# Where the outputs of a two-layer matmul kernel stand on chip, and how its last outputs leave it

## The chip, the cores and the metric

The kernel runs on one core of one Trainium2 chip. The metric is the device time of one execution in microseconds (us). Every ratio is the mean time of one kernel's runs over that of the other's of the same rounds, so it is not quite the ratio of the medians quoted beside it. A profile is of one execution. Its span leaves out some 1.6 us of that execution's time (900.2 of 901.8 us before).

## The reference

```python
x: (16, 512, 768)   w1: (768, 3072)   b1: (3072)   w2: (3072, 768)      # float32
y = np.maximum(np.matmul(x, w1) + b1, 0)
return np.matmul(y, w2).astype(np.float32)
```

## The kernel before

The 8192 rows of x are taken in eight blocks of 1024. The hidden dimension is cut into two chunks of 1536, so there are 16 block passes ("it" 0 to 15): first all eight blocks with chunk 0, then all eight with chunk 1. Passes are called blocks 0 to 15 below. Both products use fast matrix multiplication schemes: seven products in place of eight for x·w1, and 20 products of sums of y and sums of w2 for y·w2. All matmuls are fp16. VectorE forms the sums, VectorE and ScalarE take the products out of PSUM.

The second product of a block is a list of 20 steps. Each "mm" is eight matmuls into two PSUM banks (q0 to q3), and what follows takes them into the buffers s0 to s5 or into one of eight outputs of 128x768 fp32. Its end:

```python
    ("mm", 10, 2, False), ("DVE", "q1", 2, 1, "s5", 1), ("DVE", "o5", 1, -1, "s2", 1),
    ("mm", 14, 0, False), ("ACT", "s4", 0, -1),
    ("mm", 9, 3, False),  ("DVE", "q1", 3, -1, "s4", 1), ("DVE", "o7", 1, 1, "s1", -1),
    ("mm", 17, 2, False), ("DVE", "o4", 2, 1, "s5", 1),
    ("mm", 0, 0, False),  ("DVE", "o1", 0, 1, "s3", -1),
    ("mm", 7, 3, False),  ("DVE", "o6", 3, -1, "s4", 1),     # o6 = s4 - q3
```

Outputs o2, o3 and o0 come earlier in the list. An output stands in one of four buffers until its store has read it. In the first eight blocks it is stored plainly. In the last eight it is added to what lies in DRAM by an accumulating store from GpSimd:

```python
        self.o_pool = pool("o", 4)
        ...
        def output(to):
            pair = {"o5": 0, "o7": 0, "o1": 1, "o6": 1}.get(to)
            if it <= self.NSB or pair is None:                    # NSB = 8
                return self.o_pool.tile([P, 2, NH], FP32, name="o")
            ...                                # blocks 9 to 15: two larger tiles for o5, o7, o1, o6
        def total(engine, to, q, sign, kept=None, kept_sign=None):
            ...
            if to[0] == "o":
                ...
                if it < self.NSB:
                    nc.sync.dma_start(out=rows, in_=o)
                else:
                    nc.gpsimd.dma_start(out=rows, in_=o, accum_op=ALU.add)
```

The next block's first product starts between the last two steps of this list. Its step p1 writes the PSUM bank that o7 was taken from. Its step p5 writes the bank that o4 was taken from, and ScalarE copies it into the buffer that the second product calls s4. Its step p3 adds onto that bank after the copy.

x stands in slots of 128x1536 fp16, four slots for the even blocks, four for the odd ones, three for sums:

```python
        self.x = self.one.tile([P, 11, 3, self.MH], FP16, name="x")
        self.s = self.one.tile([P, 6, self.N], FP32, name="s")
```

Of the kernel before, what the change touches and what calls it, by code (L numbers as in the profile page):

```python
# [9 lines left out]
FP32 = mybir.dt.float32  # L10
# [3 lines left out]
ALU = mybir.AluOpType  # L14
# [4 lines left out]
P = 128  # L19
# [20 lines left out]
U_OF = (A1, A3, D106, D102, A10, A4, A2, A11, A0, A7, D103, A5, D101, A6, D105, U15, A9, A8,  # L40
        D104, D100)
# [108 lines left out]
class Fast:  # L150
# [440 lines left out]
        return [p1, p5, p6, p2, p7, p3, p4]  # L591


    def second(self, it):

        nc = self.nc
        QM, NH = self.QM, self.NH
        row0 = (it % self.NSB) * 2 * self.MH

        def product(p, q, start):  # L600
            for s in range(4):
                for j in range(2):
                    m0 = s * QM + j * P
                    nc.tensor.matmul(self.ps[:, 2 * q + j, 0:NH],  # L604
                                     lhsT=self.y[:, U_OF[p], m0:m0 + P],
                                     rhs=self.v[:, V_OF[p], s, :], start=(start and s == 0),
                                     stop=(s == 3), skip_group_check=True)

        def at(name):
            if name[0] == "q":  # L610
                q = int(name[1])
                return self.ps[:, 2 * q:2 * q + 2, 0:NH]
            return self.s[:, int(name[1])].rearrange("p (a n) -> p a n", a=2)

        pairs = {}

        def output(to):

            pair = {"o5": 0, "o7": 0, "o1": 1, "o6": 1}.get(to)
            if it <= self.NSB or pair is None:  # L620
                return self.o_pool.tile([P, 2, NH], FP32, name="o")
            if pair not in pairs:
                pairs[pair] = [self.raw_pool.tile([P, 4, NH], FP32, name="o2", tag="raw"), 0]
            half = pairs[pair][1]
            pairs[pair][1] = 2
            return pairs[pair][0][:, half:half + 2]

        def total(engine, to, q, sign, kept=None, kept_sign=None):
            ps = at(f"q{q}")
            o = output(to) if to[0] == "o" else at(to)  # L630
            if kept is None:
                if engine == "ACT":
                    nc.scalar.activation(out=o, in_=ps, func=ACTF.Copy, scale=float(sign))  # L633
                else:
                    nc.vector.tensor_scalar(out=o, in0=ps, scalar1=float(sign), scalar2=None,
                                            op0=ALU.mult)
            else:
                a, b = (ps, at(kept)) if sign > 0 else (at(kept), ps)
                nc.vector.tensor_tensor(out=o, in0=a, in1=b,  # L639
                                        op=ALU.add if sign == kept_sign else ALU.subtract)  # L640
            if to[0] == "o":
                r, n = divmod(int(to[1]), 2)
                rows = self.of[row0 + r * QM:row0 + (r + 1) * QM, n * NH:(n + 1) * NH]
                rows = rows.rearrange("(j p) n -> p j n", p=P)
                if it < self.NSB:
                    nc.sync.dma_start(out=rows, in_=o)
                else:
                    nc.gpsimd.dma_start(out=rows, in_=o, accum_op=ALU.add)  # L648

        steps = []  # L650
        for what in SECOND:
            if what[0] == "mm":
                steps.append([lambda a=what[1:]: product(*a)])
            else:
                steps[-1].append(lambda a=what: total(*a))
        return [lambda fns=fns: [fn() for fn in fns] for fns in steps]
# [92 lines left out]
    def plan(self):  # L749

        TP, NSB, NIT = self.TP, self.NSB, self.NIT
        self.hooks = {}
        vector = self.nc.vector

        def put(kind, it, q, i, fn, *args):
            self.hooks.setdefault((kind, it, q, i), []).append(lambda: fn(*args))


        put("p1", 0, 1, 1, self.transpose_x_first, 1)
        for s in range(4):  # L760
            put("p1", 0, 2, s, self.square_x, 0, 0, s, True)
            put("p1", 0, 1, 2, self.square_x, 0, 1, s)
        put("p1", 0, 1, 2, self.load_x, 1, (1,))
        put("p1", 0, 4, 1, self.transpose_x, 1, 0)
        put("p1", 0, 5, 1, self.transpose_x, 1, 1)
        put("m2", 0, 0, 3, self.save_x, 0, 0)
        for t, at in enumerate(((1, 1), (1, 2), (2, 0), (2, 2), (3, 1), (4, 0))):
            put("p1", 0, *at, lambda t: self.sums_w1(self.w1s[t], vector, (0, 1, 2)), t)
        for t in range(TP):
            put("m2", 0, 0, 8 + t, lambda t: self.sums_w1(self.w1s[t], vector, (3,)), t)  # L770
        for n in range(15):
            put("p1", 0, 2 + n // 8, n % 8 // 2, self.sum_w2, n, 0, 2)
            late = {10: 3, 12: 4, 14: 5, 13: 6, 11: 7}.get(n)
            at = ("m2", 0, 0, late) if late else ("p1", 0, 4 + (n + 2) // 8, (n + 2) % 8 // 2)
            put(*at, self.sum_w2, n, 2, 4)
        put("m2", 0, 0, 12, self.sum_w2, 15)

        for it in range(NIT):
            nxt = it + 1
            if nxt < NSB:  # L780
                for half in range(2):
                    if it:
                        put("m1", it, 2 + half, 0, self.transpose_x, nxt, half)
                    for s in range(4):
                        put("m2", it, 0, 1 + 4 * half + s, self.square_x, nxt, half, s)
                if nxt + 1 < NSB:
                    put("m2", it, 0, 5, self.load_x, nxt + 1, (0,))
                    put("m2", it, 0, 9, self.load_x, nxt + 1, (1,))
                put("m1", nxt, 1, 0, self.save_x, nxt, 1)
                put("m1", nxt, 4, 0, self.save_x, nxt, 0)  # L790
            elif nxt < NIT:
                put("m1", it, 4 if nxt == NSB + 1 else 2, 4, self.fetch_x, nxt, 0)
            if nxt <= NSB:
                for n, i in enumerate((6, 7, 14)):
                    put("m2", it, 0, i, self.sums_x, nxt, n)
            elif nxt < NIT:
                put("m2", it, 0, 1, self.fetch_x, nxt, 1)

        last = NSB - 1
        for t in range(TP):  # L800
            for step, at in enumerate((("m2", 1 + t, 0, 1), ("m2", 1 + t, 0, 13),
                                       ("m1", 2 + t, 0, 3))):
                put(*at, self.ahead_w1, 1 + t, t, step)
            put("m1", last, t, 6, self.fetch_w1, t)
        for n in range(12):
            put("m1", 1 + n // 3, 3 + n % 3, 0, self.load_w2,
                self.w2dram.rearrange("p b (s n) -> p b s n", s=4)[:, n // 4 * 2:][:, 0:2], 1,
                n // 4, n % 4)
        for q, at in ((2, ("m1", last, 1, 6)), (0, ("m1", last, 3, 6)), (1, ("m2", last, 0, 1))):
            put(*at, self.fetch_w2_aside, q)  # L810
        put("m2", last, 0, 9, self.fetch_w2, B0)
        put("m2", last, 0, 13, self.fetch_w2, B2)
        for n, at in ((2, ("m2", last, 0, 12)), (6, ("m2", last, 0, 14)),
                      (1, ("m2", last, 0, 16)), (15, ("m2", last, 0, 17)),
                      (9, ("m2", last, 0, 17)), (7, ("m2", last, 0, 18)),
                      (3, ("m1", NSB, 0, 3)), (0, ("m1", NSB, 1, 1)), (8, ("m1", NSB, 1, 2)),
                      (4, ("m1", NSB, 1, 3)), (5, ("m1", NSB, 2, 1)), (12, ("m1", NSB, 2, 3)),
                      (10, ("m2", NSB, 0, 5)), (14, ("m2", NSB, 0, 6)),
                      (13, ("m2", NSB, 0, 11)), (11, ("m2", NSB, 0, 14))):
            put(*at, self.sum_w2, n)  # L820

        for t in range(TP):
            for n in range(3):
                put("m2", 1 + t, 0, 11 + 3 * n, self.stat_w1, 0, t, n)
                put("m2", NSB + t // 2, 0, 3 + 9 * (t % 2) + 2 * n, self.stat_w1, 1, t, n)
        for n in range(8):
            put("m1", 2 + n // 2, 2 + 2 * (n % 2), 3, self.stat_w2, 0, n // 2, n % 2)
            put("m1", NSB + 1 + n // 4, 1 + n % 4, 3, self.stat_w2, 1, n // 2, n % 2)
        for stage in range(3):
            put("m1", NSB + 3 + stage, 5, 6, self.out_of_range, stage)  # L830
# [51 lines left out]
```

## Time and profile before

| | before |
|---|---|
| time, four runs | 901.62, 902.07, 904.03, 906.7 us |
| span and granted TensorE clock of the profile | 900.2 us, 0.994 |
| TensorE busy | 868.4 us (96%) |
| last matmul to the end of the span | 14.2 us |

L536 is the first product (L604 is the second). Timelines give start, duration, engine, line, operation, operands, count, and idle time before. One matmul of L536 shows 379 ns (the profile works out the ends of matmuls by a model; their starts are measured), though they start 0.216 us apart: each overlaps the next. TensorE's timeline at the end of block 0 (start, duration, engine, line, operation, operands, count, and idle time before) shows it:

```profile
71.90 0.81 PE L536 MATMUL ps<-x,w1s 128*128 128x512 f16 x3 [0.25 <-DVE o L639]
72.54 1.46 PE L604 MATMUL ps<-v,y 128*128 128x384 f16 x8
73.84 2.75 PE L536 MATMUL ps<-x,w1s 128*128 128x512 f16 x12
78.60 2.75 PE L536 MATMUL ps<-x,w1s 128*128 128x512 f16 x12 [2.00 <-ACT s L544]
```

### The profile page before, as it was taken

How to read it: one execution, taken by the hardware profiler on the slowest of the kernel's cores; microseconds unless marked ns; L12 is line 12 of the kernel's file. 1: busy time of each engine (PE TensorE's matmuls, PEld its weight loads, DVE VectorE, ACT ScalarE, POOL GpSimd, SP SyncE). 2: the span in 40 equal slices, each digit the busy share in tenths (PEclk: the TensorE clock that was granted, in tenths of full speed). 3: DMA queues.
4: the chain of work that ended last, by engine and by line, in shares of the span. 5: the costliest groups of instructions: out<-in, count | busy, mean ns of one | idle time of the engine just before them, and what ended most of it. 6: DMA issues, size and time to landing. Idle time of an engine off the chain costs nothing.

```text
span 900.2 us, 12564 instructions
## 1 busy us (share of the span) xinstructions
PE 868.4 (96%) x4677; PEld 458.1 (51%) x4677; DVE 618.4 (69%) x1081; ACT 519.5 (58%) x791; POOL 190.9 (21%) x173
## 2 busy tenths in 40 slices
PE   8998999999999999999989999999999999999993
PEld 6454554545445455454545545455454545545452
DVE  2896856768577675866798666676766668576663
ACT  4764757757577675666346586775626354362630
POOL 6210150501404032040200401203030130402113
PEclk9999999999999999999999999999999999999997
DMA  9999498795986959539543716639273573815418
GB/s 205 199 209 261 101 230 231 117 274 125 268 191 136 263 109 262 134 142 348 226 168 140 110 32 160 104 125 138 76 126 63 155 109 123 125 38 93 81 19 124
DMA packets 120325, 138.11 MB, mean 153 GB/s; under 512 B 67116, under 2 KB 113732, under 8 KB 116420
## 3 DMA queue, kind: packets, MB, share of 16 engines
q0 software_dynamic: 50672, 46.41, 36.5%
q1 hardware_dynamic: 69264, 90.06, 30.4%
q8 instruction: 38, 0.62, 0.3%
q10 hardware_dynamic: 324, 0.80, 0.3%
q14 instruction: 27, 0.22, 0.1%
HBM read 72.17 MB, written 77.66 MB: 166 GB/s over the span
## 4 chain that ended last, share of the span: by engine, by line
PE 40%; issue 36%; POOL 9%; DVE 6%; DMA 6%; ACT 2%; POOLq 0%; DVEq 0%; ACTq 0%
PE ps L536 23%; PE ps L604 18%; POOL out_dram L648 8%; DMA out_dram<-o 3%; DVE o L639 3%; DMA v<-in_w_dram 2%; DVE ps L639 1%; DVE v L338 1%; DMA w1s<-in_w_dram 1%; ACT s L633 1%; ACT s L544 1%; POOL w1s L277 1%; DVE y L468 0%; DVE w1s L285 0%; DVE x L391 0%
## 5 line engine op out<-in xcount | busy, mean ns | idle before, releaser
L536 PE MATMUL ps<-x,w1s 128*128 128x512 f16 x1890 | 416.2, 379 | 11.7 <-ACT s L544 8.8
L604 PE MATMUL ps<-v,y 128*128 128x384 f16 x2560 | 424.6, 326 | 2.5 <-DVE y L468 1.9
L604 PEld LDWEIGHTS <-y 128*128 128x128 f16 x2560 | 249.5, 98 | 174.4 <-ACT y L553 2.5
L536 PEld LDWEIGHTS <-w1s 128*128 128x128 f16 x1890 | 184.8, 98 | 232.4 <-issue 15.4
L544 ACT ACTIVATE s<-ps,b1y 128x512 f32<-128x512 f32 x210 | 142.0, 687 | 162.4 <-DVE y L548 53.9
L468 DVE TENSOR_TENSOR y<-y 128x512 f16<-128x512 f16 x512 | 201.8, 420 | 32.9 <-ACT y L553 25.6
L548 DVE CUSTOM_DVE_ANT_0 y<-ps,s 128x512 f16<-128x512 f32 x210 | 145.0, 690 | 107.4 <-PE ps L536 73.2
L648 POOL DMA_DIRECT2D out_dram<-o x64 | 77.8, 1380 | 366.0 <-DVE o L639 366.0
L633 ACT ACTIVATE s<-ps 128x768 f32<-128x768 f32 x96 | 77.7, 810 | 121.2 <-PE ps L604 96.7
L639 DVE TENSOR_TENSOR o<-s,ps 128x768 f32<-128x768 f32 x64 | 61.0, 953 | 60.1 <-PE ps L604 26.7
L639 DVE TENSOR_TENSOR s<-ps,s 128x768 f32<-128x768 f32 x96 | 90.2, 954 | 12.5 <-ACT s L633 6.5
L553 ACT ACTIVATE y<-ps,b1y 128x512 f16<-128x512 f32 x90 | 61.9, 687 | 39.7 <-PE ps L536 39.7
L639 DVE TENSOR_TENSOR o<-ps,s 128x768 f32<-128x768 f32 x64 | 58.8, 953 | 36.8 <-ACT s L633 34.9
L394 POOL TENSOR_TENSOR x<-x 128x3072 f16<-128x3072 f16 x7 | 42.1, 6009 | 65.7 <-DVE x L391 53.1
L382 ACT ACTIVATE scrap<-xn 128x768 f16<-128x768 f16 x60 | 50.3, 838 | 0.8
L277 POOL DMA_DIRECT2D x<-in_w_dram x12 | 10.1, 848 | 182.7 <-PE ps L536 182.7
L559 ACT ACTIVATE ps<-ps,b1y 128x512 f32<-128x512 f32 x60 | 39.6, 659 | 10.8 <-PE ps L536 7.9
L553 ACT ACTIVATE y<-ps 128x512 f16<-128x512 f32 x60 | 35.8, 597 | 0.0
L346 ACT ACTIVATE scrap<-scrap 128x1536 f16<-128x1536 f16 x24 | 35.4, 1477 | 0.1
L633 ACT ACTIVATE ps<-ps 128x768 f32<-128x768 f32 x32 | 25.5, 798 | 9.2 <-PE ps L604 8.9
L486 PE MATMUL ps<-x,w1s 128*128 128x512 f16 x132 | 28.8, 379 | 0.4 <-DVE x L441 0.2
L369 POOL DMA_DIRECT2D xn<-in_x_dram x15 | 11.5, 764 | 74.3 <-ACT scrap L382 73.5
(64 smaller groups left out, 260.2 us busy)
## 6 DMA issues: line engine op xcount, KB each, us to landing
out_dram<-o SPq DMA_DIRECT2D x64, 384.0 KB, 4.3
out_dram<-o POOLq DMA_DIRECT2D x64, 384.0 KB, 5.8
xd<-x SPq DMA_DIRECT2D x8, 1536.0 KB, 5.4
x<-xd SPq DMA_DIRECT2D x8, 1536.0 KB, 8.4
xn<-in_x_dram POOLq DMA_DIRECT2D x15, 768.0 KB, 7.3
xd<-x SPq DMA_DIRECT2D x7, 1152.0 KB, 7.0
x<-xd SPq DMA_DIRECT2D x7, 1152.0 KB, 5.3
w1d<-x SPq DMA_DIRECT2D x6, 672.0 KB, 5.3
```

The costliest lines, as they stand in the source:

```text
L382: self.nc.scalar.activation(out=self.junk(self.K), in_=rows, func=ACTF.Square, accum_out=self.stat[:, i:i + 1])
L394: (self.nc.gpsimd if it > 1 else self.nc.vector).tensor_tensor(out=x[:, a21:self.XS2 + 1:self.XS2 - a21], in0=x[:, a21:self.XS1 + 1:self.X ...
L468: self.nc.vector.tensor_tensor(out=pair(*outs), in0=pair(*ins0), in1=pair(*ins1), op=ALU.add if sign > 0 else ALU.subtract)
L536: nc.tensor.matmul(ps, lhsT=w[:, slot, k, :], rhs=x[:, xslot, k, :], start=(start and k == 0), stop=(k == 2), skip_group_check=True)
L544: nc.scalar.activation(out=kept(name), in_=ps, func=ACTF.Identity, bias=bias)
L548: nc.vector._custom_dve(TENSOR_ADD_SAT, out=self.y_of(self.TP * half + t, m), in0=self.two(ps), in1=self.two(kept(name)), s0=F_MAX, s1=0.0)
L553: nc.scalar.activation(out=self.y_of(self.TP * half + t, m), in_=self.two(ps), func=ACTF.Relu, **kw)
L559: nc.scalar.activation(out=g["b"], in_=g["a"], func=ACTF.Identity, bias=bias1)
L604: nc.tensor.matmul(self.ps[:, 2 * q + j, 0:NH], lhsT=self.y[:, U_OF[p], m0:m0 + P], rhs=self.v[:, V_OF[p], s, :], start=(start and s == 0) ...
L633: nc.scalar.activation(out=o, in_=ps, func=ACTF.Copy, scale=float(sign))
L639: nc.vector.tensor_tensor(out=o, in0=a, in1=b, op=ALU.add if sign == kept_sign else ALU.subtract)
L648: nc.gpsimd.dma_start(out=rows, in_=o, accum_op=ALU.add)
```

## The change

Its intent is threefold: to have no output wait for a buffer in blocks 0 to 8, to take VectorE's other work out of the crowded places, and to end the program with plain stores. Two of eight outputs of a block (o5, o4) are put into slots of x that the block no longer needs. For four of the eight last outputs the part of chunk 0 is loaded from DRAM beforehand and added by GpSimd to the s buffer that the output will be formed from, so these leave by plain stores. The last output is split into halves on two queues.

```diff
+    def x_outputs(self, slot):
+        o = self.x[:, slot].rearrange("p k m -> p (k m)").bitcast(FP32)
+        return o.rearrange("p (a n) -> p a n", a=2)
+    LAST = {"o7": ("s1", -1, 3), "o4": ("s5", 1, 15), "o1": ("s3", -1, 12), "o6": ("s4", 1, 16)}
+    def fetch_last(self, to):                    # slot = index in LAST
+        self.nc.sync.dma_start(out=self.x_outputs(slot), in_=self.rows_of(self.NIT - 1, to))
+    def add_last(self, to):
+        self.nc.gpsimd.tensor_tensor(out=s, in0=s, in1=self.x_outputs(slot),
+                                     op=ALU.add if sign > 0 else ALU.subtract)
 ...
         def output(to):
+            slot = {"o5": 2, "o4": 3}.get(to)
+            if it <= self.NSB and slot is not None:
+                return self.x_outputs(4 * (it % 2) + slot)
 ...
+            if final and to == SECOND[-1][1]:
+                for j, queue in enumerate((nc.scalar, nc.sync)):
+                    nc.vector.tensor_tensor(out=o[:, j], in0=at(kept)[:, j], in1=ps[:, j], op=ALU.subtract)
+                    queue.dma_start(out=self.rows_of(it, to)[:, j], in_=o[:, j])
+                return
 ...
-                if it < self.NSB:
+                if it < self.NSB or (final and to in self.LAST):
                     nc.sync.dma_start(out=rows, in_=o)
 ...
-        for t, at in enumerate(((1, 1), (1, 2), (2, 0), (2, 2), (3, 1), (4, 0))):    # sums of w1
+        for t, at in enumerate(((1, 1), (1, 2), (2, 0), (2, 2))):
+        for t in (4, 5):
+            put("m1", 1, t - 3, 3, lambda t: self.sums_w1(self.w1s[t], vector), t)
 ...   # and the fourth sum of these two strips no longer in block 0's second product
-                for n, i in enumerate((6, 7, 14)):
-                    put("m2", it, 0, i, self.sums_x, nxt, n)
+                put("m2", it, 0, 6, self.sums_x, nxt, 0)
+                put("m2", it, 0, 7, self.sums_x, nxt, 1)
+                put("m1", nxt, 0, 0, self.sums_x, nxt, 2)                # this is L399
 ...   # sums of w2 for chunk 1, six of them moved:
-  (6, ("m2", last, 0, 14)), (1, ("m2", last, 0, 16)), (9, ("m2", last, 0, 17)), (7, ("m2", last, 0, 18))
+  (6, ("m1", NSB, 1, 0)),   (1, ("m1", NSB, 4, 3)),   (9, ("m2", NSB, 0, 1)),   (7, ("m2", NSB, 0, 3))
-  (13, ("m2", NSB, 0, 11)), (11, ("m2", NSB, 0, 14))
+  (13, ("m2", NSB, 0, 9)),  (11, ("m2", NSB, 0, 12))
+        for to, (_, _, i) in self.LAST.items():
+            put("m1", NIT - 1, 1, 6, self.fetch_last, to)
+            put("m2", NIT - 1, 0, i, self.add_last, to)
```

More of the change, by code (lines that the diff above doesn't have):

```diff
@@ L591, in first, with rows_of @@
         return [p1, p5, p6, p2, p7, p3, p4]
+    def rows_of(self, it, to):
+        r, n = divmod(int(to[1]), 2)
+        m0 = (it % self.NSB) * 2 * self.MH + r * self.QM
+        rows = self.of[m0:m0 + self.QM, n * self.NH:(n + 1) * self.NH]
+        return rows.rearrange("(j p) n -> p j n", p=P)
+    def x_outputs(self, slot):
[3 more added lines that the diff above has]
+    def fetch_last(self, to):
+        slot = list(self.LAST).index(to)
+        self.nc.sync.dma_start(out=self.x_outputs(slot), in_=self.rows_of(self.NIT - 1, to))
+    def add_last(self, to):
+        slot = list(self.LAST).index(to)
+        name, sign, _ = self.LAST[to]
+        s = self.s[:, int(name[1])].rearrange("p (a n) -> p a n", a=2)
+        self.nc.gpsimd.tensor_tensor(out=s, in0=s, in1=self.x_outputs(slot),
+                                     op=ALU.add if sign > 0 else ALU.subtract)
     def second(self, it):
@@ L597, in second @@
         QM, NH = self.QM, self.NH
-        row0 = (it % self.NSB) * 2 * self.MH
+        final = it == self.NIT - 1
         def product(p, q, start):
-            for s in range(4):
-                for j in range(2):
-                    m0 = s * QM + j * P
-                    nc.tensor.matmul(self.ps[:, 2 * q + j, 0:NH],
-                                     lhsT=self.y[:, U_OF[p], m0:m0 + P],
-                                     rhs=self.v[:, V_OF[p], s, :], start=(start and s == 0),
-                                     stop=(s == 3), skip_group_check=True)
+            order = [(s, j) for s in range(4) for j in range(2)]
+            if final and p == SECOND[-2][1]:
+                order.sort(key=lambda sj: sj[1])
+            for s, j in order:
+                m0 = s * QM + j * P
+                nc.tensor.matmul(self.ps[:, 2 * q + j, 0:NH],
+                                 lhsT=self.y[:, U_OF[p], m0:m0 + P],
+                                 rhs=self.v[:, V_OF[p], s, :], start=(start and s == 0),
+                                 stop=(s == 3), skip_group_check=True)
         def at(name):
@@ L630, in total @@
             o = output(to) if to[0] == "o" else at(to)
+            if final and to == SECOND[-1][1]:
+                for j, queue in enumerate((nc.scalar, nc.sync)):
+                    nc.vector.tensor_tensor(out=o[:, j], in0=at(kept)[:, j], in1=ps[:, j],
+                                            op=ALU.subtract)
+                    queue.dma_start(out=self.rows_of(it, to)[:, j], in_=o[:, j])
+                return
             if kept is None:
@@ L641, in total @@
             if to[0] == "o":
-                r, n = divmod(int(to[1]), 2)
-                rows = self.of[row0 + r * QM:row0 + (r + 1) * QM, n * NH:(n + 1) * NH]
-                rows = rows.rearrange("(j p) n -> p j n", p=P)
-                if it < self.NSB:
+                rows = self.rows_of(it, to)
+                if it < self.NSB or (final and to in self.LAST):
                     nc.sync.dma_start(out=rows, in_=o)
@@ L766, in plan @@
         put("m2", 0, 0, 3, self.save_x, 0, 0)
-        for t, at in enumerate(((1, 1), (1, 2), (2, 0), (2, 2), (3, 1), (4, 0))):
+        for t, at in enumerate(((1, 1), (1, 2), (2, 0), (2, 2))):
             put("p1", 0, *at, lambda t: self.sums_w1(self.w1s[t], vector, (0, 1, 2)), t)
-        for t in range(TP):
             put("m2", 0, 0, 8 + t, lambda t: self.sums_w1(self.w1s[t], vector, (3,)), t)
+        for t in (4, 5):
+            put("m1", 1, t - 3, 3, lambda t: self.sums_w1(self.w1s[t], vector), t)
         for n in range(15):
@@ L812, in plan @@
         put("m2", last, 0, 13, self.fetch_w2, B2)
-        for n, at in ((2, ("m2", last, 0, 12)), (6, ("m2", last, 0, 14)),
-                      (1, ("m2", last, 0, 16)), (15, ("m2", last, 0, 17)),
-                      (9, ("m2", last, 0, 17)), (7, ("m2", last, 0, 18)),
+        for n, at in ((2, ("m2", last, 0, 12)), (6, ("m1", NSB, 1, 0)),
+                      (1, ("m1", NSB, 4, 3)), (15, ("m2", last, 0, 17)),
+                      (9, ("m2", NSB, 0, 1)), (7, ("m2", NSB, 0, 3)),
                       (3, ("m1", NSB, 0, 3)), (0, ("m1", NSB, 1, 1)), (8, ("m1", NSB, 1, 2)),
@@ L818, in plan @@
                       (10, ("m2", NSB, 0, 5)), (14, ("m2", NSB, 0, 6)),
-                      (13, ("m2", NSB, 0, 11)), (11, ("m2", NSB, 0, 14))):
+                      (13, ("m2", NSB, 0, 9)), (11, ("m2", NSB, 0, 12))):
             put(*at, self.sum_w2, n)
+        for to, (_, _, i) in self.LAST.items():
+            put("m1", NIT - 1, 1, 6, self.fetch_last, to)
+            put("m2", NIT - 1, 0, i, self.add_last, to)
         for t in range(TP):
```

## The prediction

> **What bounds the kernel now.** I read the busy table of the page first, then the waits of TensorE, then the timeline around each place where TensorE stands still.
>
> ```profile
> PE 868.4 (96%) x4677; PEld 458.1 (51%) x4677; DVE 618.4 (69%) x1081; ACT 519.5 (58%) x791; POOL 190.9 (21%) x173
> ```
>
> TensorE is the bound: 868.4 of 900.2 us busy at a granted clock of 0.994, and the change neither adds nor removes a matmul. So only its 31.8 us of idle time can be won. The view of waits of TensorE splits up most of it, and one line of the same view for all engines names the root:
>
> ```profile
> PE ps L536 <- ACT s L544: 8.8, 6, 2.0
> PE ps L536 <- DVE o L639: 2.9, 9, 1.1
> PE ps L604 <- DVE y L468: 1.9, 1, 1.9
> ...
> DVE o L639 <- DMA out_dram<-o: 7.9, 6, 2.2
> ```
>
> The first two lines, 8.8 + 2.9 = 11.7 us, are the first matmuls of the next block's first product (L536). TensorE's timeline places them at the nine block boundaries of blocks 0 to 8: 2.25, 1.36, 0.98, 1.78, 0.18, 0.53, 0.18, 2.93 and 1.47 us. At the boundaries of blocks 9 to 14 it shows none. VectorE's timeline at the end of block 0 shows how such a stall arises:
>
> ```profile
> 69.03 0.95 DVE L399 TENSOR_TENSOR x<-x 128x1536 f16<-128x1536 f16 x1
> 69.90 0.95 DVE L639 TENSOR_TENSOR ps<-s,ps 128x768 f32<-128x768 f32 x1
> 70.89 0.96 DVE L639 TENSOR_TENSOR o<-ps,s 128x768 f32<-128x768 f32 x1
> 72.00 0.96 DVE L639 TENSOR_TENSOR o<-ps,s 128x768 f32<-128x768 f32 x1 [0.15 <-DMA out_dram<-o]
> 74.12 0.96 DVE L639 TENSOR_TENSOR o<-ps,s 128x768 f32<-128x768 f32 x1 [1.17 <-DMA out_dram<-o]
> 76.21 0.95 DVE L639 TENSOR_TENSOR o<-s,ps 128x768 f32<-128x768 f32 x1 [1.13 <-DMA out_dram<-o]
> ```
>
> A block has eight outputs and the pool has four buffers, so the last four (o7, o4, o1, o6) wait until the first four have been stored. The last, o6, frees the buffer s4; ScalarE's copy L544 into it comes next, and then TensorE's p3, which adds onto that bank. In block 9, which has neither the wait nor the operation L399, o6 ends at 567.62, the copy at 568.43, and p3 is due at 569.07 (12 matmuls of 0.216 us after 566.47): about 0.6 us of slack. Any output buffer that comes later than that is paid by TensorE.
>
> The third line, 1.9 us at 49.95, is the start of block 0's second product: VectorE is busy 13.72 of the 14 us before 45, and a sum of y comes late.
>
> The end is the third place. VectorE's last output ends at 886.97, GpSimd issues the last accumulating stores until 889.4, and:
>
> ```profile
> 884.47 4.94 POOL L648 DMA_DIRECT2D out_dram<-o  x4 [0.88 <-DVE o L639]
> 886.02 0.95 DVE L639 TENSOR_TENSOR o<-s,ps 128x768 f32<-128x768 f32 x1
> ...
> out_dram<-o POOLq DMA_DIRECT2D x2, 384.0 KB, 9.7
> ```
>
> The page's median for accumulating stores is 5.8 us from issue to landing; the last two take a median of 9.7 because four queue up at the 171 to 184 GB/s that the DMA view shows from 884 to 896. The last was issued at 887.3 and took 10.4 us (the maximum in the tile's view), so it landed at 897.7, 2.5 us before the end of the span.
>
> **What the Trainium skill says.** "DMA: Bandwidth & Descriptors", section "SWDGE vs HWDGE vs iDMA": accumulation during a DMA can be issued from GpSimd alone, plain transfers from SP or ACT. The kernel before is built so. The same page, section "Specifications", gives about 358 GB/s of HBM per core; plain stores in a quiet stretch of this trace (396 to 397 and 401 to 404) move 356 to 367 GB/s and land in 2.4 to 2.9 us, twice the rate of the accumulating ones. "GPSIMD Engine Reference", section "Elementwise — side-by-side cycle accounting": a two-input add of 2048 fp32 elements takes 4497 ns, 2.2 ns each. The trace has 6009 ns for 3072 fp16 elements and 916 for 384, a line of 1.895 ns per element plus 188 ns, which agrees roughly. "SBUF — State Buffer", section "Who interferes with whom": VectorE blocks a reading GpSimd when both its inputs are in SBUF. In the tail every VectorE operation has one input in PSUM, so I expect no such block there; no trace so far shows it.
>
> **The change, part by part.**
>
> 1. *Two of eight outputs in slots of x (blocks 0 to 8).* o5 and o4 go to x slots whose last reader is the block's own first product. Six outputs on four buffers: o7 takes the fourth buffer, o1 takes o2's (11 products of 1.3 us, some 14 us, earlier) and o6 takes o3's (9 products). Against landings of 2.4 to 8.5 us no output waits any more. The slot's other users are far: the copy of x to DRAM is issued at 51.43 and takes 12.1 us at worst, against an o5 at about 66; the transposes into it come over 15 us after the store.
>
> 2. *Operation L399 (0.95 us, 8 times) moves from before o7 to between o1 and o6.* This takes the recurring 0.18 us off the wait for o7's bank. It now stands before o6, but in the last block o1 ends about 1.25 us after its product does, and o6's product, with three matmuls of L536 between, ends 1.95 us after o1's, so L399 (0.87 us from start to start) delays o6 by 0.1 to 0.2 us, and the slack is 0.6.
>
> 3. *w2 sums of block 7 and 8.* Boundary 7 has four 0.95 us sums (L338) between its last outputs; all four leave, two to each product of block 8, and the sums of block 8 are pulled ahead of o5. Boundaries 7 and 8 then look like block 9's. The price is about 1.9 us more of VectorE in block 8's first product (it had 2.8 us of idle in 475 to 484) and 1.9 us early in its second product, where I count slack of 0.7 to 1.9 us before each need. I leave 0.3 us for a residual stall.
>    Parts 1 to 3 together: 11.7 - 0.3 = 11.4 us.
>
> 4. *Six w1 sums (L285's two groups at 36.03 and 40.34, 1.13 + 1.14 = 2.27 us) leave the crowded start* for block 1's first product. The sum that TensorE awaited until 49.95 comes at about 47.7, and TensorE is there at 47.9 to 48.1. The waits of 1.89 and 0.17 us go: 2.0 us.
>
> 5. *The tail.* Four outputs get the first chunk's part added on chip beforehand and leave by plain stores. The four adds run on GpSimd, an estimate of 768 x 1.895 + 188 = 1.64 us each from the trace's line. Two are early. The other two stand behind o5's accumulating store, which ends at 882.38 + 1.20 = 883.58: the add for o4 ends at about 885.25 and that for o6 at 886.9. So VectorE's o4, at 884.1 before, starts at 885.35; o1 follows until 887.2, then o6 in two halves (0.55 us each, as the 128x384 cast from PSUM at 558 ns) until about 888.15. That is 1.2 us *later* than now. The final half is issued at 888.25. Ahead of it in the DMA engines are o4, o1 and the first half, at 1.07 us per 384 KB (393 KB at 367 GB/s); issue to first byte is about 1 us. Data: o4 887.4 to 888.4, o1 to 889.5, o6 to 890.6, landed at about 891.0. Plus the 2.5 us: 893.5 in place of 900.2, a gain of 6.7 us. The loads of the first chunk's rows (four of 384 KB) lie some 40 us before, beside matmuls.
>
> Sum: 11.4 + 2.0 + 6.7 = 20.1 us, so 904.0 - 20 = 884.0 us, 2.2% less.
>
> **Rivals.**
> (a) *The adds on GpSimd become the tail.* If they cost twice the estimate (the skill's rate is for fp32, mine from fp16), o4 and o6 come 3.3 us later and the tail wins 3.5 us in place of 6.7: about 887.5 us. For it: GpSimd is serial and stands behind a 1.2 us issue. Against: two sources agree on 1.65 us.
> (b) *The store wait was hidden by another one.* Should ScalarE's copy or VectorE's own queue be the real limit at a boundary, stalls would stay. The blocks 9 to 14, free of both, show none; blocks 4 and 6, with L399 but quiet stores, show 0.18. So this can keep 2 to 4 us at most: about 887.
> (c) *The moved sums become a new stall.* Block 8's VectorE is 82% busy between 460 and 512. A lag of over 1 us would show in L604 waiting for L338 or L468: 1 to 3 us, 886.
> (d) *More is won.* The median lies 2.3 us above the profiled run's 901.8. If that surplus is slow stores, it goes too: about 881.5.
>
> **Range and chances.** The limit for 2% is 885.95, only 2 us above my number. Three of four rivals lose time and each costs about 2 to 3.5 us; all together would still be a gain of 1%. I take 884.0 with 880.5 to 888.5; faster by over 2% 0.66, within 2% 0.33, slower 0.01.
>
> **What will show it.** Right: no VectorE wait for out_dram; L536 waiting under 1 us in all; no L604 wait near 48 us; GpSimd adds of about 1.6 us; last landing near 5 us after the last matmul rather than 11.7. Wrong: L536 still waiting for L544 at boundaries, adds over 2.5 us, new L604 waits in block 8, or an accumulating store of o5 that lands last.

## More of the kernel before

Besides the lines that the prediction shows, this group of the page matters. It has its line, engine, operation, output and input, their shapes and the count, then busy time and the mean of one in ns, then how long the engine stood still just before them and what ended most of that.

```profile
L536 PE MATMUL ps<-x,w1s 128*128 128x512 f16 x1890 | 416.2, 379 | 11.7 <-ACT s L544 8.8
```

## The result, and the profile after

| | before | after |
|---|---|---|
| time, median of four runs | 903.05 us (901.62 to 906.7) | 880.57 us (880.3 to 881.02) |
| ratio, 95% interval | | 0.9746 (0.9715 to 0.9777) |
| span and clock of the profile | 900.2 us, 0.994 | 879.4 us, 0.996 |
| start of the first block's following product (first p1) | 71.90 us | 69.36 us |
| first p1 to last p1 (block 0's end to block 14's end) | 759.42 us | 746.60 us |
| last p1 to the last matmul | 54.66 us | 54.66 us |
| last matmul to the end of the span | 14.2 us | 8.8 us |

The gain in the profile is 20.8 us, and the last four rows split it: 2.5 + 12.8 + 0 + 5.4. The lines that answer to those of before, first the page's engines and TensorE's two groups (L604 is now L633):

```profile
PE 866.2 (98%) x4677; PEld 458.1 (52%) x4677; DVE 619.3 (70%) x1082; ACT 518.8 (59%) x791; POOL 193.3 (22%) x173
...
L633 PE MATMUL ps<-v,y 128*128 128x384 f16 x2560 | 424.6, 326 | 1.0 <-ACT ps L672 0.6
L536 PE MATMUL ps<-x,w1s 128*128 128x512 f16 x1890 | 415.6, 379 | 0.0
```

The 11.7 us before L536 are gone entirely, and no wait of VectorE for a store is left in the view of waits. TensorE's busy time fell by 2.2 us with the same matmuls: that is about what the ends of matmuls come to that had been counted where a wait followed (15 x 0.163 = 2.4).

VectorE's timeline at the end of block 0, after the change (its output lines are L678 now):

```profile
67.06 0.96 DVE L678 TENSOR_TENSOR ps<-s,ps 128x768 f32<-128x768 f32 x1
68.05 0.96 DVE L678 TENSOR_TENSOR o<-ps,s 128x768 f32<-128x768 f32 x1
68.93 0.94 DVE L678 TENSOR_TENSOR x<-ps,s 128x768 f32<-128x768 f32 x1
69.79 0.95 DVE L678 TENSOR_TENSOR o<-ps,s 128x768 f32<-128x768 f32 x1
70.66 0.94 DVE L399 TENSOR_TENSOR x<-x 128x1536 f16<-128x1536 f16 x1
71.52 0.94 DVE L678 TENSOR_TENSOR o<-s,ps 128x768 f32<-128x768 f32 x1
```

These are q1, o7, o4 (into a slot of x), o1, L399 and o6, back to back, where before three of them waited for DMAs. o6 starts 2.16 us after p1 did (69.36), against 4.31 before. TensorE's timeline there has no idle time:

```profile
69.36 0.81 PE L536 MATMUL ps<-x,w1s 128*128 128x512 f16 x3
...
71.31 9.01 PE L536 MATMUL ps<-x,w1s 128*128 128x512 f16 x41
```

The tail, in the timeline of the changed kernel. The last matmul ends at 870.62:

```profile
867.01 1.20 POOL L685 DMA_DIRECT2D out_dram<-o  x1 [0.85 <-DVE o L678]
867.77 4.04 POOL L618 TENSOR_TENSOR s<-s,x 128x768 f32<-128x768 f32 x2
...
868.90 3.41 SPq L683 DMA_DIRECT2D out_dram<-o  x3
870.09 1.82 DVE L678 TENSOR_TENSOR o<-ps,s 128x768 f32<-128x768 f32 x2 [1.22 <-POOL s L618]
871.85 1.02 DVE L666 TENSOR_TENSOR o<-s,ps 128x384 f32<-128x384 f32 x2
872.43 0.38 ACTq L668 DMA_DIRECT2D out_dram<-o  x1
872.89 0.34 SPq L668 DMA_DIRECT2D out_dram<-o  x1
```

o5's accumulating store and the two adds stand one behind the other on GpSimd, and VectorE's o4 waits 1.22 us for the first of them. In the windows (stretch, its length, busy time of PE, PEld, DVE, ACT and POOL, granted clock, share of the 16 DMA engines, GB/s) the transfers run without a break until 876 and trail off after it:

```profile
870.00:871.00 1.00, 0.62 (x4) 0.17 (x2) 0.91 (x2) 0.00 (x0) 1.00 (x2) 1.00 0.98 160
...
872.00:873.00 1.00, 0.00 (x0) 0.00 (x0) 0.87 (x2) 0.00 (x0) 0.00 (x0) 0.85 1.12 393
...
875.00:876.00 1.00, 0.00 (x0) 0.00 (x0) 0.00 (x0) 0.00 (x0) 0.00 (x0) 0.50 0.96 349
876.00:877.00 1.00, 0.00 (x0) 0.00 (x0) 0.00 (x0) 0.00 (x0) 0.00 (x0) 0.50 0.35 72
```

While o5's accumulating store is under way the rate is 160 to 177 GB/s (868 to 871), and from 872 to 876 it is 349 to 393. The DMA view tells whose packets these are. It gives the queue, its packets, MB and share of the 16 engines; GpSimd's queue is "software_dynamic", SP's "hardware_dynamic". First 870 to 871, then 871 to 873:

```profile
q0 software_dynamic: 104, 0.16, 98.4%
...
q1 hardware_dynamic: 306, 0.45, 61.3%
q0 software_dynamic: 124, 0.17, 48.5%
```

The plain store of o7 was issued at 868.90, but no packet of SP's queue is listed before 871. It stood behind o5's accumulating store for 2 us.

### The profile page after: what moved, and what is told of

Its sections match the earlier page's. It is cut to its first block, busy times and chain, and to the rows that moved or that the text cites. A ratio compares the mean times of both kernels' runs of the same rounds, so it can differ in the third digit from the quotient of the medians. Undisturbed runs are those within 1.5% of the kernel's fastest.

```text
span 879.4 us, 12571 instructions
## 1 busy us (share of the span) xinstructions
PE 866.2 (98%) x4677; PEld 458.1 (52%) x4677; DVE 619.3 (70%) x1082; ACT 518.8 (59%) x791; POOL 193.3 (22%) x173
## 4 chain that ended last, share of the span: by engine, by line
PE 50%; issue 35%; POOL 9%; DVE 3%; DMA 2%; ACT 0%; POOLq 0%; DVEq 0%; ACTq 0%
PE ps L536 25%; PE ps L633 25%; POOL out_dram L685 8%; DVE v L338 1%; DMA v<-in_w_dram 1%; DMA w1s<-in_w_dram 1%; DVE y L468 1%; POOL s L618 1%; POOL w1s L277 1%; DVE o L678 0%; ACT ps L672 0%; DVE w1s L285 0%; DVE ps L678 0%; DVE x L678 0%; DVE x L391 0%
## 5 line engine op out<-in xcount | busy, mean ns | idle before, releaser
L633 PE MATMUL ps<-v,y 128*128 128x384 f16 x2560 | 424.6, 326 | 1.0 <-ACT ps L672 0.6
L536 PE MATMUL ps<-x,w1s 128*128 128x512 f16 x1890 | 415.6, 379 | 0.0
L633 PEld LDWEIGHTS <-y 128*128 128x128 f16 x2560 | 249.6, 98 | 173.0 <-ACT y L553 2.5
L536 PEld LDWEIGHTS <-w1s 128*128 128x128 f16 x1890 | 184.8, 98 | 218.6 <-issue 0.9
L544 ACT ACTIVATE s<-ps,b1y 128x512 f32<-128x512 f32 x210 | 142.1, 686 | 149.7 <-PE ps L536 69.2
L685 POOL DMA_DIRECT2D out_dram<-o x58 | 71.2, 1363 | 327.9 <-DVE o L678 327.9
L678 DVE TENSOR_TENSOR s<-ps,s 128x768 f32<-128x768 f32 x96 | 90.1, 952 | 11.6 <-ACT s L672 5.6
L678 DVE TENSOR_TENSOR o<-s,ps 128x768 f32<-128x768 f32 x54 | 51.3, 950 | 48.3 <-PE ps L633 25.9
L678 DVE TENSOR_TENSOR o<-ps,s 128x768 f32<-128x768 f32 x55 | 51.3, 953 | 37.0 <-ACT s L672 35.1
```

Of the source, the lines that this page charges most:

```text
L536: nc.tensor.matmul(ps, lhsT=w[:, slot, k, :], rhs=x[:, xslot, k, :], start=(start and k == 0), stop=(k == 2), skip_group_check=True)
L544: nc.scalar.activation(out=kept(name), in_=ps, func=ACTF.Identity, bias=bias)
L633: nc.tensor.matmul(self.ps[:, 2 * q + j, 0:NH], lhsT=self.y[:, U_OF[p], m0:m0 + P], rhs=self.v[:, V_OF[p], s, :], start=(start and s == 0) ...
L678: nc.vector.tensor_tensor(out=o, in0=a, in1=b, op=ALU.add if sign == kept_sign else ALU.subtract)
```

## The experiments

Eleven kernels ran, in three jobs. The first four ran on one chip, the other seven on another. All gave correct results. The kernel before ran beside each: a median of 901.87 us over 11 runs in the first job, and 902.29 us over 9 runs in each of the other two, which share eight of them.

| run | span | time, median | ratio to before |
|---|---|---|---|
| last stores only | 895.1 | 896.70 | 0.9951 |
| all but the last stores | 884.9 | 886.33 | 0.9829 |
| slots of x only | 892.0 | 893.70 | 0.9912 |
| changed, o5 plain too | 877.9 | 879.51 | 0.9752 |
| changed, L399 back | 881.7 | 883.33 | 0.9793 |
| changed, w2 sums back | 883.3 | 885.25 | 0.9809 |
| changed, w1 sums back | 880.9 | 883.04 | 0.9790 |
| changed, o5's store last | 880.8 | 882.34 | 0.9782 |
| changed, again | 879.1 | 880.79 | 0.9764 |
| changed, last output whole | 878.6 | 880.43 | 0.9761 |
| changed, three additions | 876.9 | 878.24 | 0.9734 |

**The last block's stores alone.** From the changed kernel, everything but the tail is undone:

```diff
-            slot = {"o5": 2, "o4": 3}.get(to)
-            if it <= self.NSB and slot is not None:
-                return self.x_outputs(4 * (it % 2) + slot)
 ...  and the hooks of sums_w1, sums_x and sum_w2 as in the kernel before
```

> Only the last block's plain stores, with their adds on GpSimd and the split last output; everything else as before. If the three parts of the change simply add up along TensorE's path, this wins the tail's 5.4 us of the profile (14.2 us from the last matmul to the end of the span become 8.8): span about 894.8, and the boundary stalls stay (L536 waiting about 11.7 us). Theory of the spread: the runs of the kernel before differ by 5 us because the store waits at the boundaries differ from run to run; then this kernel still spreads by 2 us or more. Rival: the spread sits in the queue of accumulating stores at the end; then this kernel is as steady as the changed one (under 1 us) and its median gains more than 5.4 us.

The span was 895.1 us, as expected, with 8.8 us from the last matmul to the end. The stalls stayed. TensorE's line of the waits and VectorE's (us in total, times, longest):

```profile
PE ps L536 <- ACT s L544: 9.0, 6, 2.2
...
DVE o L675 <- DMA out_dram<-o: 8.3, 6, 2.2
```

The six runs were 895.28, 895.85, 896.63, 896.76, 897.58 and 901.79 us: even without the outlier they spread by 2.3 us, so the spread did not leave with the last four accumulating stores.

**All but the last block's stores.**

```diff
-        final = it == self.NIT - 1
+        final = False
-    LAST = {"o7": ("s1", -1, 3), "o4": ("s5", 1, 15), "o1": ("s3", -1, 12), "o6": ("s4", 1, 16)}
+    LAST = {}
```

> The changed kernel with the last block as before: four accumulating stores at the end and no adds. Additive: span about 879.4 + 5.4 = 884.8, no boundary stalls. Theory of the spread (boundary waits): steady, within 1 us over the runs. Rival (spread in the accumulating stores at the end): spreads by 2 us or more.

The span was 884.9 us, so the tail and the rest add up. Last matmul to end: 14.0 us. The runs were 885.83 to 887.37 us, a spread of 1.5 us, a little over what was expected but well under that of the kernels with store waits.

**Two outputs in slots of x, alone.** To the kernel before is added only:

```diff
         def output(to):
+            slot = {"o5": 2, "o4": 3}.get(to)
+            if it <= self.NSB and slot is not None:
+                return self.x_outputs(4 * (it % 2) + slot)
```

> The kernel before with only o5 and o4 in slots of x. Theory: the waits of VectorE for out_dram (7.9 us) vanish; left are 0.18 + 0.16 us at the boundaries 0 to 6 and 8 (L399 still ahead of o7), 0.3 to 0.5 more at boundary 5, and some 3.2 us at boundary 7 with its four w2 sums: about 6.3 of the 14.1 us that the boundaries cost in TensorE's start times. Gain about 7.7 us, span about 892.5. Rival: the store wait hid another limit; then the copies L544 still hold L536 at boundaries 0 to 3 and the gain is under 4 us.

The span was 892.0 us, a gain of 8.2. VectorE's waits for out_dram vanished. Of L536's waits for L544 one was left, 1.9 us, at boundary 7 with its four w2 sums:

```profile
PE ps L536 <- DVE o L678: 2.8, 9, 1.1
...
PE ps L536 <- ACT s L544: 1.9, 1, 1.9
```

From p1 to p1 the blocks now take 53.57 to 53.62 us, which is still 0.35 more than with the whole change, and that is L399 ahead of o7. The five runs lie within 0.9 us. So the wait for the buffers was the cause of the stalls at boundaries 0 to 3 and 8, with no other limit behind it. It also seems to be most of what varied from run to run, though five runs against the eleven of the kernel before (900.47 to 903.46) show that only roughly.

**L399 back in its old place.**

```diff
-                put("m1", nxt, 0, 0, self.sums_x, nxt, 2)
+                put("m2", it, 0, 14, self.sums_x, nxt, 2)
```

> The changed kernel with L399 (the third sum of x) back in its old place ahead of o7's chain, outputs still in slots of x. If a stall costs TensorE its listed idle time plus 0.16 us of a matmul that runs out alone, the eight boundaries 0 to 7 each cost 0.18 + 0.16 = 0.34 us again: L536 waits 1.4 us in all but the span grows by 2.7 us, to about 882.1. Rival (the listed idle time is the whole cost, as the prediction had it): 1.4 us, 880.8.

The span was 881.7, the median 2.5 us above that of the changed kernel (883.33 against 880.79). The changed kernel was timed again in the third job and not in this one, but on the same chip; this holds for the next three comparisons too. TensorE's waits are those expected:

```profile
PE ps L536 <- DVE o L678: 1.4, 7, 0.2
...
PE ps L536 <- DMA out_dram<-x: 0.2, 1, 0.2
```

The eighth wait is put down to a store from a slot of x, but its block is no longer than the others. The lines sum to 1.6 us, but TensorE's last p1 came at 818.77 against 815.96, 2.8 us later, which is 0.35 for each of eight boundaries. So a wait costs what is listed (0.18 us) and 0.16 us more.

**The w2 sums back.**

```diff
-  (6, ("m1", NSB, 1, 0)), (1, ("m1", NSB, 4, 3)), (9, ("m2", NSB, 0, 1)), (7, ("m2", NSB, 0, 3)) ... (13, ..., 9), (11, ..., 12)
+  (6, ("m2", last, 0, 14)), (1, ("m2", last, 0, 16)), (9, ("m2", last, 0, 17)), (7, ("m2", last, 0, 18)) ... (13, ..., 11), (11, ..., 14)
```

> The changed kernel with the w2 sums of blocks 7 and 8 in their old places. Boundary 7 gets its four sums back: in the run with slots alone the two periods around it were 54.46 and 55.58 us against 53.19 and 53.90 in the changed kernel, so the span grows by 1.27 + 1.68 = 2.95 us to about 882.3, and L536 waits about 2.9 us. Boundary 8 stays free, since its wait came from the store and not from the sums. Rival: boundary 8's old stall came from its sums; then it comes back too and the span is 883.5 or more.

This cost more than expected: 883.3 us of span and 4.5 us of median. Boundary 8 took back only 0.18 us, so the rival does not explain it. Part of the surplus is that L399 now stands between the four sums and o6, so that the stall at boundary 7 is 2.75 us in place of 1.88. The rest is another thing, seen in TensorE's timeline and in the windows after the stall:

```profile
444.38 2.75 PE L536 MATMUL ps<-x,w1s 128*128 128x512 f16 x12
449.88 6.38 PE L536 MATMUL ps<-x,w1s 128*128 128x512 f16 x21 [2.75 <-ACT s L544]
...
450.00:455.00 5.00, 5.00 (x16) 1.89 (x15) 3.11 (x4) 1.78 (x4) 0.00 (x0) 0.66 0.09 33
455.00:460.00 5.00, 5.00 (x25) 2.25 (x24) 3.96 (x6) 3.15 (x5) 0.00 (x0) 1.00 0.18 32
```

The granted clock fell to 0.66 in 450 to 455, and TensorE started 16 matmuls there where the next five us have 25. The 105 matmuls after the stall take 24.51 us, against 22.82 after the shorter stall of the kernel before: 1.7 us for the clock. Of the five runs four had a mean clock of 0.995 or 0.996 and 884.83 to 885.65 us, and one had 0.998 and 883.40 us. The Trainium skill, "TensorE: Matmul & The Clock Gate", section "What's actually happening", has a free-running window of about 3.4 us and half the clock after one idle window. The drop to about half is what this trace shows (weight loads 0.43 us apart in place of 0.216), but here a pause of 2.75 us was enough. The stalls of up to 2.0 us in the kernel before, and of 2.2 us in the run with the last stores only, show a clock of 1.00.

**The w1 sums back.**

```diff
-        for t in (4, 5):
-            put("m1", 1, t - 3, 3, lambda t: self.sums_w1(self.w1s[t], vector), t)
+  ... (2, 2), (3, 1), (4, 0)   and the fourth sum of t = 4, 5 in block 0's second product
```

> The changed kernel with the six w1 sums back at the crowded start. The wait of 1.9 us before block 0's second product returns (0.23 us is left of it in the changed kernel), with 0.2 us for another one and 0.16 us for each; and nothing is gained in block 1: span 879.4 + 2.1 = 881.5 (881.2 to 881.9). Rival: VectorE catches up in block 0 and the boundary 0 hides it: under 1 us.

The median was 883.04, 2.25 us above the changed kernel. The first p1 came at 71.67 in place of 69.36, and the span (880.9) grew less because the tail happened to be 0.9 us shorter. The waits of 1.9 us for a sum of y and 0.5 us for a w2 sum were back. So the gain of this part is not hidden by later slack.

**o5 of the last block by a plain store as well.**

```diff
-    LAST = {..., "o6": ("s4", 1, 16)}
+    LAST = {..., "o6": ("s4", 1, 16), "o5": ("s2", 1, 6)}
-            put("m1", NIT - 1, 1, 6, self.fetch_last, to)
+            put(*(("m2", NIT - 1, 0, 1) if to == "o5" else ("m1", NIT - 1, 1, 6)), self.fetch_last, to)
```

> The changed kernel with a fifth output of the last block (o5) handled like the other four: its first part is fetched into a fifth slot of x once the last first product is over, added to s2 early in the second product, and it leaves by a plain store. GpSimd then has no store to issue between the products of o4 and o6, so its two late adds start about 2 us earlier and VectorE's o4 waits less or not at all; the last DMAs share with one accumulating store fewer. If GpSimd's queue holds the tail: the last VectorE operation comes 1.4 us sooner and the span is about 878. If the transfers hold it: o5's 384 KB takes 1.1 us in place of 2.2, span about 878.3. If neither does (only the fixed time after the last landing): no change, 879.4.

The span was 877.9 us: 1.5 us less than the changed kernel's 879.4, and from the last matmul to the end 7.1 us in place of 8.8. VectorE's o4 no longer waits and its last operation ends 1.2 us earlier. In medians the difference is about 1.1 us (879.51 against 880.57; the changed kernel did not run in this job). The tail of the changed kernel itself is not that steady: 8.8 us in its first profile, 8.5 in its second, and 7.9 to 8.8 in the four experiments with the same last stores (last stores only, L399, w2 sums, w1 sums). This run alone can't tell whether GpSimd's order or the transfers had been the limit. The next one was made for that.

**o5's accumulating store after the adds.** The store is kept as it was, but GpSimd issues it once both late adds are done:

```diff
+                if final and to == "o5":
+                    self.late = lambda: nc.gpsimd.dma_start(out=rows, in_=o, accum_op=ALU.add)
+                    return
 ...
+        put("m2", NIT - 1, 0, 16, lambda: self.late())         # after the add for o6
```

> The changed kernel with o5's accumulating store of the last block issued after GpSimd's two late adds in place of before them. VectorE's o4 and o6 then have their adds in time and the last half is issued about 1.3 us sooner, but the accumulating store is issued 3 us later. If the order on GpSimd holds the tail: span about 878, as with o5 by a plain store. If the transfers hold it (the DMA engines are busy without a break from the last product on): no gain or a loss, 879.4 to 880.5.

VectorE's last operation now ends 0.9 us after the last matmul, in place of 2.25, exactly as with the plain o5. Yet the span was 880.8, a little above the 879.4 to 880.5 that were expected for limiting transfers, and the median 882.34, 1.55 us above the changed kernel. The windows show why:

```profile
870.00:871.00 1.00, 0.77 (x5) 0.25 (x3) 1.00 (x2) 0.00 (x0) 1.00 (x1) 1.00 1.02 366
...
872.00:873.00 1.00, 0.00 (x0) 0.00 (x0) 0.00 (x0) 0.00 (x0) 0.00 (x0) 1.00 1.01 117
...
876.00:877.00 1.00, 0.00 (x0) 0.00 (x0) 0.00 (x0) 0.00 (x0) 0.00 (x0) 0.50 1.01 319
```

The plain stores ran at 366 GB/s, and as soon as the accumulating one joined them everything fell to between 117 and 269. That store took 8.7 us to land, and the half output issued beside it on ScalarE's queue 6.5. So the transfers hold the tail here. What GpSimd's order is worth by itself this run doesn't measure, because it moved the store along with the order. For the changed kernel the answer is argued from its trace: plain stores began to move only at 871 and then ran at the full rate until 876, so an o4 issued 1.2 us earlier (in place of 871.07) would have stood behind o7 all the same.

**The last output whole.**

```diff
-            if final and to == SECOND[-1][1]:
+            if False:                              # and the eight matmuls in their old order
```

> The changed kernel with its last output in one piece: one subtraction of 128x768 and one store of 384 KB on SP in place of two halves on two queues, products in the old order. If the transfers hold the tail, the DMA engines are busy with o4 and o1 anyway when the first half would start: no change within 0.4 us. If the last store's own issue and landing hold it: 0.5 us or more later.

880.43 us against 880.79 in the same rounds, with overlapping runs (880.08 to 881.34 and 880.63 to 881.08). Splitting the last output brings nothing that these runs can show, which agrees: the DMA engines have enough to do while it is being formed.

**The changed kernel again.**

> The changed kernel itself, for a second measurement beside the two below and beside more runs of the kernel before. In two jobs the kernel before had medians of 901.9 and 902.3 us (20 runs, 900.5 to 903.5), while its first three timed runs had 904.0. If the first three were an unlucky draw, the gain here is 21 to 22 us and the ratio 0.976 to 0.977; if the gain of 22.5 us and the ratio of 0.9746 stand, it is more than the profile's 20.8 us shows and something is still missing.

The median was 880.79 us over five runs (880.63 to 881.08), the ratio 0.9764. The kernel before had 902.29. The gain is 21.5 us, so the first comparison's 22.5 had an unlucky draw of the kernel before in it.

**Three additions to the changed kernel.**

```diff
  ... LAST with "o5" as above, and
-            (14, ("m2", NSB, 0, 6)),
+            (14, ("m2", NSB, 0, 8)),
-        for t in (4, 5):
+        for t in (3, 4, 5):
             put("m1", 1, t - 3, 3, lambda t: self.sums_w1(self.w1s[t], vector), t)
```

> The changed kernel with three small additions: o5 of the last block by a plain store (879.5 us by itself), the w2 sum for V14 in block 8 two products later (it stands ahead of o2 and makes TensorE wait 0.40 us; the period of block 8 is 53.90 us against 53.19 elsewhere, so 0.7 us), and the w1 sums of a third strip out of the crowded start (0.23 us of wait left there plus 0.16). If these add up: 879.5 - 0.7 - 0.4 = 878.4 us, span about 876.8, and TensorE waits for no sum of y or w2. Rival: the moved sum meets its product late, or block 1 is now too full: no gain over 879.5.

878.24 us (878.08 to 878.43), span 876.9: what the sum of the three had given, and every run faster than every run of the changed kernel. The period of block 8 fell from 53.90 to 53.33 us, the first p1 from 69.32 to 68.88, and TensorE waits for no sum of y or w2 any more. It beats both kernels: 2.55 us less than the changed one, 24.05 less than the one before, in the same rounds.

## Why the prediction was right or wrong

The mechanism held in parts 1 to 4; in part 5 the path of the transfers was wrong. The time did not hold: 884.0 us was forecast and 880.57 came. That is at the very edge of the range, whose lower end was 880.5: the median lies 0.07 us inside, while the ratio of 0.9746 times the 903.05 us of the kernel before gives 880.1, outside. Three terms were mis-sized, and not all in the same direction.

**The base.** The step that failed most is "904.0 - 20 = 884.0". The 20 us were read off the trace of a run of 901.8 us and then subtracted from the median of three runs, 904.03, one of which had taken 906.7. In some 20 later runs the kernel before lay between 900.5 and 903.5 us. Of the 3.4 us between 884.0 and 880.57, 904.03 - 901.8 = 2.2 come from there. Another 0.45 are luck: the profiled run of the changed kernel was the slowest of its four. The remaining 0.8 are the terms below (20.8 us in place of 20). Rival (d) had named the first of these and came near with 881.5; I gave it too little weight. (The difference is 2.2 and not the 2.3 of rival (d), which makes it 881.8; rival (a)'s 6.7 - 3.3 is 3.4 and its time 887.3. Nothing hangs on either.) The runs with parts of the change suggest that the variation sat largely in the waits for output buffers: the kernels that had the waits spread by 2.3 us or more, those without by 0.4 to 1.5 (the one with the dips of the clock aside). That the three runs had 904.0 in the middle was, beside that, an unlucky draw. What made the one run of 901.79 us slow was not profiled and stays open.

**The boundaries (parts 1 to 3)** were put at 11.4 us and gave 13.2 (12.8 from p1 to p1, and 0.41 in the first p1 itself). Each stall costs TensorE the idle time that the waits list and a matmul's end of 0.163 us that nothing covers. That is the 379 ns of the group's line less the 216 ns from start to start. The Trainium skill, "TensorE: Matmul & The Clock Gate", section "Single matmul latency", has the same (398 + 512) / 2.4 = 379 ns for one alone. The sum "8.8 + 2.9 = 11.7" therefore lacked 15 x 0.16 = 2.4 us. The residual, put at 0.3 us, was 0.9: 0.7 of it in block 8, where a w2 sum ahead of o2 held TensorE for 0.40 us, and the three additions removed most of that (0.57 us of the block's period). Rival (c) thus happened, smaller than its 1 to 3 us.

**The start (part 4)**, 2.0 us, gave 2.1: the 1.89 became 0.23 rather than nothing, the 0.17 went, one matmul end of 0.16 went with it, and the waits for w1 before them happened to be 0.1 us shorter. That it agrees with the forecast is thus partly luck.

**The tail (part 5)** was put at 6.7 us and gave 5.4. VectorE's part was right almost to the tenth: o4 was to wait 1.25 us and waited 1.22, and the last half was to end 2.2 us after the last matmul and ended 2.25 after it. Two errors cancel there: the adds took 1.9 us alone and 2.0 in a row rather than 1.64 (no run shows why; it is nowhere near rival (a)'s double), but in GpSimd's records, which are rough, the first of the two begins at 867.77, before the store's record ends at 868.21. What failed is the list of transfers "ahead of it in the DMA engines: o4, o1 and the first half". It left out o5's accumulating store, which was still under way and landed at 872.73, and o7, which stood behind it: o7 took 4.8 us to land in place of 2.4 to 2.9, and the full rate came only after 871. The last landing that the trace records (o1, at 877.03) came 6.4 us after the last matmul, where 5.0 were forecast; that is where the missing 1.3 us went. The experiment with the later o5 store shows the accumulating store slowing the plain ones beside it directly. Part of the 1.3 us may be chance, since 8.8 us is the longest tail of the six profiles with these stores (the shortest has 7.9).

Together: 13.2 + 2.1 + 5.4 = 20.7 of the 20.8 us. Rival (b) is out: with the slots alone, no store wait was left and nothing held the boundaries but L399 (0.18 us each) and, at boundary 7, the four w2 sums, which parts 2 and 3 had named.

One point that the prediction left open showed up in the changed kernel's timeline, at the early add for o7. The columns are as before:

```profile
848.42 1.90 POOL L618 TENSOR_TENSOR s<-s,x 128x768 f32<-128x768 f32 x1 [27.61 <-DVE s L678]
848.58 2.03 DVE L468 TENSOR_TENSOR y<-y 128x512 f16<-128x512 f16 x1
```

A sum of y that takes 0.42 us elsewhere took 2.03, and it ended 0.29 us after GpSimd's add did. Both its inputs are in SBUF and GpSimd had started 0.16 us before it, so this fits the blocking that the prediction quotes from the skill's SBUF page, here with VectorE as the one that waits. The same sum took 2.03 us in the changed kernel's second profile too; no experiment moved it away. TensorE was not held by it. In the tail, where each of VectorE's operations reads PSUM, they kept 0.95 us beside the adds, as the prediction expected.

## What to carry to other kernels

A wait for a free output buffer can be removed without more memory where another tile has just been read for the last time; look for what follows the freed buffer in the chain, since here it was the next product's PSUM copy and not the store that TensorE felt. When the idle time of a pipelined engine is summed from waits, add one uncovered end per wait (0.163 us here), and subtract from the time of the run that was profiled. At the end of a program count all transfers in flight, accumulating ones at about half the rate (here 171 to 184 GB/s against 356 to 367) and as a brake on the plain ones beside them, and don't polish the order of the engines before the transfers.

## What the Trainium skill lacked or had wrong

- "DMA: Bandwidth & Descriptors" says that accumulation needs GpSimd, but not what it costs. Here a plain 384 KB store lands in 2.4 to 2.9 us when nothing else runs and moves 356 to 367 GB/s. An accumulating one takes 5.0 to 5.4 us, and a queue of them moves 171 to 184. All stores together fell from 366 to between 117 and 269 GB/s when one joined, and a plain store issued while one was under way moved nothing for 2 us.
- "TensorE: Matmul & The Clock Gate" gives the latency of a single matmul and says that one alone cannot hide its drain, but no page that I found says that a stall in a trace therefore costs TensorE one uncovered end (0.163 us for 512 columns) on top of the idle time listed. From the first p1 to the second it was 2.50 us for two stalls of 2.18 us listed.
- The same page asks for no pause over some 3 us and names an idle window of about 3.4. A pause of 2.75 us was followed by 1.7 us lost at about half clock, in four of five runs going by their mean clock, while pauses of up to 2.2 us left it at 1.00.
- "GPSIMD Engine Reference", section "Elementwise — side-by-side cycle accounting", held roughly: 2.2 ns per element would make 1.7 us of the 768-element fp32 add, an estimate from the page's figure, and the trace has 1.9 to 2.0.
